# Gather, running sum and matrix product: sums and carry per tile of 128 rows in place of pairs of 256

## Chip, cores, metric

One core of one Trainium2 chip. The metric is the device time of one execution in microseconds (us), median of the runs of a kernel. The runs were spread over several chips, and the same kernel differs between them by up to 1.2%, so every kernel is compared only with runs of the kernel before on the same chip.

## The reference

```python
B, S, N, D = 16, 4096, 2048, 512
# x: (B, S, D) float32; indices: (B, N) sorted int64; w: (D, D) float32
def reference(x, indices, w):
    gathered = x[np.arange(B)[:, None], indices, :].copy()
    cs = np.cumsum(gathered, axis=1)
    return np.matmul(cs, w).astype(np.float32)
```

That is 16 x 2048 = 32768 gathered rows, 256 tiles of 128 rows, 128 pairs of tiles.

## The kernel before

Five engines work as a chain, each with its own list of instructions, coupled by semaphores:

- GpSimd gathers one tile of 128 rows per instruction (fp32 in HBM, fp16 in the core's memory) into a ring of 16 tiles. It may overwrite a pair's buffers when TensorE (PE) has signalled (`s_a`) that this pair's sums are done.
- PE multiplies the gathered tile with a triangle of ones. That gives the running sums within a tile or pair, already transposed (`sums`).
- VectorE adds the last column of the pair before to the sums and casts them to fp16 (`carry`, signal `s_d`).
- PE multiplies the carried sums with w (`project`, signal `s_b`).
- ScalarE copies the product out of PSUM (`drain`, signal `s_e`), and SyncE stores it.

Cuts from the kernel (its constants drawn together in the first line, comments added, left-out lines as `...`):

```python
R, NG, NA, NB, NC, NO, AH = 2, 16, 2, 2, 4, 8, 2   # AH: pairs that sums run ahead of project
...
def gather(t):
    g, r = divmod(t, R)
    pool.need(s_a, g + 1 - NG // R)            # wait: sums of the pair 8 earlier are done
    ...
    nc.gpsimd.indirect_dma_start(
        out=g16[g % (NG // R)][:, r, :], out_offset=None, in_=x_flat,
        in_offset=bass.IndirectOffsetOnAxis(ap=ap, axis=0),
        element_offset=(t // NT) * S * D,
    ).then_inc(s_g[t % NG], 16)

def sums(t):
    g, r = divmod(t, R)
    pe.need(s_g[t % NG], 16 * (t // NG + 1))
    pe.need(s_d, g - NA + 1)
    for c in range(DC):
        if r == 0 and c == 1:
            pe.need(s_e, g - AH - NB + 1)      # the drain of the pair four earlier
        mm = nc.tensor.matmul(
            out=pa[g % NA][:, c] if r == 0 else pa[g % NA][:, c, :, Q:],
            lhsT=g16[g % (NG // R)][:, r, c * P : (c + 1) * P],
            rhs=ut[:] if r == 0 else ut[:, :, :Q], ...)
    if r == R - 1:
        mm.then_inc(s_a, 1)
...
for g in range(1, G - AH - 1):                 # PE's steady loop
    for j in range(R):
        sums(R * (g + AH) + j)
        project(g, j)
```

The first tile of a pair writes 256 columns (both halves of the pair, since its rows count for all later ones), the second adds its 128. So a pair's sums are 4 x 256 + 4 x 128 = 1536 columns.

## Time and profile before

| | before |
|---|---|
| time, median of 3 | 404.81 us |
| span of the profiled run, mean granted clock | 403.2 us, 0.976 |
| PE busy | 324.4 us, 80% |
| GpSimd busy, all but 1.3 us of it gathers | 241.6 us, 60% |
| last gather issued | 375.57 us |

PE is the busiest engine, but a fifth of the span is not PE work.

### The profile page before, as it was taken

To read this page: it belongs to the slowest core of one execution; us is meant where nothing else is said; L and a number is where in the kernel's file an instruction comes from. 1 tells how busy PE (TensorE), PEld (TensorE's weight loads), DVE (VectorE), ACT (ScalarE), POOL (GpSimd) and SP (SyncE) were. 2 spreads that over 40 slices of the span, in tenths; PEclk is the share of its full clock that TensorE was granted. 3 is DMA by queue.
4 is the path that set the end of the run, shared out by engine and by line. 5 is a ranking of instruction groups with operands and counts; after the bars stand their busy time and mean duration, and the time that the engine had idled before them with its cause. 6 is when DMAs were issued, how large, how long until landed. Compare 5 with 4: busy or idle time off the path is not lost.

```text
span 403.2 us, 5096 instructions
## 1 busy us (share of the span) xinstructions
PE 324.4 (80%) x2064; PEld 182.4 (45%) x2064; DVE 159.2 (39%) x136; ACT 131.8 (33%) x132; POOL 241.6 (60%) x264
## 2 busy tenths in 40 slices
PE   5617988878888887888888788888878888888893
PEld 2303544444444444444444444444444444444451
DVE  2212443344444334434333443443344343433541
ACT  2102433333334333343333433343333333333442
POOL 6774666566666656666665666666566666666100
PEclk9867999999999999999999999999999999999998
DMA  7996999999999999999999999999999999999954
GB/s 175 140 128 111 278 262 262 280 272 270 259 283 257 272 269 269 279 255 284 256 275 264 278 268 266 277 258 271 267 278 271 257 284 264 277 251 281 287 227 191
DMA packets 56871, 102.32 MB, mean 254 GB/s; under 512 B 6800, under 2 KB 39824, under 8 KB 56848
## 3 DMA queue, kind: packets, MB, share of 16 engines
q0 software_dynamic: 36864, 33.57, 58.2%
q1 hardware_dynamic: 19712, 68.43, 44.2%
q8 instruction: 16, 0.26, 0.3%
q10 hardware_dynamic: 272, 0.00, 0.0%
q14 instruction: 7, 0.06, 0.0%
HBM read 68.42 MB, written 67.11 MB: 336 GB/s over the span
## 4 chain that ended last, share of the span: by engine, by line
PE 79%; issue 15%; DVE 2%; DMA 2%; ACT 0%; SPq 0%; ACTq 0%
PE pb L156 58%; PE pa L128 22%; DVE cst L146 2%; DMA g<-in_x_dram,idx_first 1%; DMA idx_first<-in_indices_dram 0%; ACT ob L168 0%; ACT ob L180 0%; ACTq L23 0%; SPq L332 0%; SPq L78 0%
## 5 line engine op out<-in xcount | busy, mean ns | idle before, releaser
L156 PE MATMUL pb<-w,cst 128*128 128x512 f16 x1024 | 266.7, 384 | 67.9 <-issue 56.6
L111 POOL DMA_INDIRECT g<-in_x_dram,idxg x252 | 236.4, 938 | 132.0 <-PE pa L128 66.3
L146 DVE TENSOR_TENSOR cst<-pa,cst 128x1024 f16<-128x1024 f32 x112 | 137.2, 1225 | 203.2 <-PE pa L128 144.8
L168 ACT COPY ob<-pb 128x1024 f32<-128x1024 f32 x127 | 128.5, 1012 | 261.9 <-remote 132.1
L156 PEld LDWEIGHTS pb<-w,cst 128*128 128x128 f16 x1024 | 94.1, 99 | 141.4 <-issue 65.8
L128 PE MATMUL pa<-ut,g 128*128 128x256 f16 (+1 forms) x1024 | 127.7, 248 | 4.3 <-DMA g<-in_x_dram,idx_first 2.7
L128 PEld LDWEIGHTS pa<-ut,g 128*128 128x128 f16 x1024 | 89.8, 99 | 69.4 <-issue 7.8
L142 DVE CAST cst<-pa 128x1024 f16<-128x1024 f32 x16 | 19.5, 1222 | 25.6 <-PE pa L128 18.4
L244 PE MATMUL pb<-zeros 128*128 128x512 f16 x14 | 5.2, 535 | 1.5 <-DVE zeros L248 1.5
L111 POOL DMA_INDIRECT g<-in_x_dram,idx_first x4 | 3.9, 986 | 2.0 <-DMA idx_first<-in_indices_dram 1.1
L244 PEld LDWEIGHTS pb<-zeros 128*128 128x128 f16 x14 | 1.7, 131 | 3.8 <-issue 1.9
L302 ACT CAST w<-w 128x512 f16<-128x512 f32 x2 | 1.2, 618 | 2.8 <-DMA w<-in_w_dram 2.8
L265 DVE CAST w<-w 128x512 f16<-128x512 f32 x2 | 0.9, 452 | 3.1 <-DMA w<-in_w_dram 3.1
L251 DVE CAST idxf<-idx 128x128 f32<-128x128 uint32 x2 | 0.5, 238 | 3.5 <-DMA idx<-in_indices_dram 3.5
L299 ACT ACT_TABLE_LOAD x1 | 1.3, 1283 | 1.5 <-SPq L78 1.5
L180 DVE COPY ob<-pb 128x512 f32<-128x512 f32 x1 | 0.7, 691 | 2.1 <-PE pb L156 2.1
L180 ACT COPY ob<-pb 128x512 f32<-128x512 f32 x1 | 0.6, 586 | 0.7 <-PE pb L156 0.7
L248 DVE MEMSET zeros<- 128x256 uint32 x1 | 0.3, 272 | 1.1 <-SPq L78 1.1
L256 PEld LDWEIGHTS pb<-ident,idxf 128*128 128x128 f32 x2 | 0.4, 187 | 0.6 <-DVE idxf L251 0.3
L262 DVE CAST idxg<-pb 128x128 uint32<-128x128 f32 x2 | 0.5, 292 | 0.2 <-PE pb L256 0.2
L256 PE MATMUL pb<-ident,idxf 128*128 128x128 f32 x2 | 0.5, 303 | 0.0
L215 POOL MEMSET ident<- 128x128 f32 x1 | 0.2, 205 | 0.5 <-SPq L78 0.5
(8 smaller groups left out, 1.6 us busy)
## 6 DMA issues: line engine op xcount, KB each, us to landing
out_dram<-ob SPq DMA_DIRECT2D x127, 512.0 KB
g<-in_x_dram,idxg POOLq DMA_INDIRECT x252
w<-in_w_dram SPq DMA_DIRECT2D x4, 256.0 KB
out_dram<-ob SPq DMA_DIRECT2D x2, 256.0 KB, 2.7
idx<-in_indices_dram SPq DMA_DIRECT2D x2, 128.0 KB, 2.6
g<-in_x_dram,idx_first POOLq DMA_INDIRECT x4
idx_first<-in_indices_dram ACTq DMA_DIRECT2D x1, 2.0 KB, 2.2
idx_first<-in_indices_dram SPq DMA_DIRECT2D x1, 2.0 KB, 2.0
```

The source lines that it names most:

```text
L111: nc.gpsimd.indirect_dma_start(out=g16[g % (NG // R)][:, r, :], out_offset=None, in_=x_flat, in_offset=bass.IndirectOffsetOnAxis(ap=ap, ax ...
L128: mm = nc.tensor.matmul(out=pa[g % NA][:, c] if r == 0 else pa[g % NA][:, c, :, Q:], lhsT=g16[g % (NG // R)][:, r, c * P : (c + 1) * P], r ...
L142: nc.vector.tensor_copy(out=dst[:], in_=pa[g % NA][:]).then_inc(s_d, 1)
L146: nc.vector.tensor_tensor(out=dst[:], in0=pa[g % NA][:], in1=last.unsqueeze(2).broadcast_to([P, DC, R, P]), op=mybir.AluOpType.add,).then_ ...
L156: mm = nc.tensor.matmul(out=pb[g % NB][:, j], lhsT=cst[g % NC][:, c, j, :], rhs=w16[:, c, :], start=(c == 0), stop=(c == DC - 1),)
L168: nc.scalar.copy(out=ob[g % NO][:], in_=pb[g % NB][:]).then_inc(s_e, 1)
L180: copy(out=ob[g % NO][:, j], in_=pb[g % NB][:, j]).then_inc(s_el[j], 1)
L244: nc.tensor.matmul(out=pb[NB - 1][:, R - 1], lhsT=zeros[:, :P], rhs=zeros[:], start=True, stop=True)
L256: nc.tensor.transpose(out=pb[k % NB][:, 0, :P], in_=idxf[:, k, :], identity=ident[:]).then_inc(s_pt, 1)
L265: nc.vector.tensor_copy(out=w16[:, c, :], in_=w32[:, c, :]).then_inc(s_wc, 1)
L299: nc.scalar.copy(out=spare[:], in_=zeros[:, :1])
L302: nc.scalar.copy(out=w16[:, c, :], in_=w32[:, c, :]).then_inc(s_wc, 1)
```

## The change

The intent is to stream fewer columns on PE. If each tile is summed on its own, the first tile of a pair no longer has to write its sums into the second tile's half: its four matmuls have 128 columns in place of 256. VectorE then carries tile by tile (twice as many adds of half the size), and the two PSUM buffers for sums become four of half the size. The core of the diff:

```diff
-    NA = 2
+    NA = 4
-    ut = const.tile([P, R, P], FP16)
+    ut = const.tile([P, R, Q], FP16)
-    pa = [ps.tile([P, DC, R, P], FP32, name=f"pa{i}") for i in range(NA)]
+    pa = [ps.tile([P, DC, R, Q], FP32, name=f"pa{i}") for i in range(NA)]
...
     def gather(t):
-        pool.need(s_a, g + 1 - NG // R)
+        pool.need(s_a, R * (g + 1) - NG)
...
     def sums(t):
-        pe.need(s_d, g - NA + 1)
+        pe.need(s_d, t - NA + 1)
...
-                out=pa[g % NA][:, c] if r == 0 else pa[g % NA][:, c, :, Q:],
+                out=pa[t % NA][:, c],
-                rhs=ut[:] if r == 0 else ut[:, :, :Q],
+                rhs=ut[:],
...
-        if r == R - 1:
-            mm.then_inc(s_a, 1)
+        mm.then_inc(s_a, 1)
-    def carry(g):
-        dve.need(s_a, g + 1)
+    def carry(t):
+        g, r = divmod(t, R)
+        dve.need(s_a, t + 1)
+        dst = cst[g % NC][:, :, :, r * Q : (r + 1) * Q]
...
     def project(g, j):
-        pe.need(s_d, min(g + 1 + j, G) if g else 1)
+        pe.need(s_d, min(R * (g + 1) + j, T))
```

More of the change, by code (lines that the diff above doesn't have):

```diff
@@ L54 @@
     AH = 2
-    assert R == 2 and D == 512 and N % (R * P) == 0 and T % P == 0
+    assert D == 512 and N % (R * P) == 0 and T % P == 0
     x_flat = x.rearrange("b s d -> (b s) d")
@@ L128, in sums @@
             mm = nc.tensor.matmul(
-                out=pa[g % NA][:, c] if r == 0 else pa[g % NA][:, c, :, Q:],
+                out=pa[t % NA][:, c],
                 lhsT=g16[g % (NG // R)][:, r, c * P : (c + 1) * P],
-                rhs=ut[:] if r == 0 else ut[:, :, :Q],
-                start=(r == 0 and c * R * P % D == 0),
-                stop=(r == R - 1 and (c + 1) * R * P % D == 0),
-            )
-        if r == R - 1:
-            mm.then_inc(s_a, 1)
-    def carry(g):
-        dve.need(s_a, g + 1)
-        dst = cst[g % NC]
-        if g % GB == 0:
-            nc.vector.tensor_copy(out=dst[:], in_=pa[g % NA][:]).then_inc(s_d, 1)
+                rhs=ut[:],
+                start=(c == 0),
+                stop=(c == DC - 1),
+            )
+        mm.then_inc(s_a, 1)
[3 more added lines that the diff above has]
+        dst = cst[g % NC][:, :, :, r * Q : (r + 1) * Q]
+        if t % NT == 0:
+            nc.vector.tensor_copy(out=dst, in_=pa[t % NA][:]).then_inc(s_d, 1)
             return
-        last = cst[(g - 1) % NC][:, :, R - 1, P - 1 : P]
-        dve.need(s_d, g)
+        e = (r - 1) % R
+        last = cst[(t - 1) // R % NC][:, :, R - 1, e * Q + Q - 1 : e * Q + Q]
+        dve.need(s_d, t)
         nc.vector.tensor_tensor(
-            out=dst[:],
-            in0=pa[g % NA][:],
-            in1=last.unsqueeze(2).broadcast_to([P, DC, R, P]),
+            out=dst,
+            in0=pa[t % NA][:],
+            in1=last.unsqueeze(2).broadcast_to([P, DC, R, Q]),
             op=mybir.AluOpType.add,
@@ L232 @@
         base=0,
-        pattern=[[1, R], [R, P]],
+        pattern=[[1, R], [R, Q]],
         channel_multiplier=-1,
@@ L265 @@
         nc.vector.tensor_copy(out=w16[:, c, :], in_=w32[:, c, :]).then_inc(s_wc, 1)
-    for g in range(G):
-        carry(g)
+    for t in range(T):
+        carry(t)
     drain_last(0, dve, nc.vector.tensor_copy)
```

## The prediction

> **What bounds the kernel now.** I read the page first (busy shares, chain, costliest groups), then the groups with shapes kept apart, then the timelines of single engines over one repeat of the steady state, then two stretches compared.
>
> ```profile
> PE 324.4 (80%) x2064; PEld 182.4 (45%) x2064; DVE 159.2 (39%) x136; ACT 131.8 (33%) x132; POOL 241.6 (60%) x264
> PE 79%; issue 15%; DVE 2%; DMA 2%; ACT 0%; SPq 0%; ACTq 0%
> ```
>
> PE is the busiest engine and 79% of the chain, yet 15% of the chain is "issue": PE idle for no reason that the profile names. So streaming columns are not all of the time. From the groups:
>
> ```profile
> L156 PE MATMUL pb<-w,cst 128*128 128x512 f16 x1024 | 266.7, 384 | 67.9 <-issue 56.6 <-DVE cst L146 11.2
> L111 POOL DMA_INDIRECT g<-in_x_dram,idxg x252 | 236.4, 938 | 132.0 <-PE pa L128 66.3 <-issue 65.7
> L146 DVE TENSOR_TENSOR cst<-pa,cst 128x1024 f16<-128x1024 f32 x112 | 137.2, 1225 | 203.2 <-PE pa L128 144.8 <-issue 41.9 <-remote 13.0
> L128 PE MATMUL pa<-ut,g 128*128 128x256 f16 x512 | 78.5, 276 | 4.1 <-DMA g<-in_x_dram,idx_first 2.7 <-issue 1.2
> L128 PE MATMUL pa<-ut,g 128*128 128x128 f16 x512 | 49.5, 219 | 0.2 <-issue 0.2
> ```
>
> PE's idle time stands before the projections (67.9 us), none before the sums: gathered data is always there in time. Where it falls is in PE's timeline, one repeat:
>
> ```profile
> 205.50 1.04 PE L156 MATMUL pb<-w,cst 128*128 128x512 f16 x4 [1.47 <-issue]
> ...
> 207.68 0.39 PE L128 MATMUL pa<-ut,g 128*128 128x128 f16 x4
> ...
> 210.06 0.39 PE L128 MATMUL pa<-ut,g 128*128 128x128 f16 x4
> ...
> 212.45 0.39 PE L128 MATMUL pa<-ut,g 128*128 128x128 f16 x4
> 214.30 1.04 PE L156 MATMUL pb<-w,cst 128*128 128x512 f16 x4 [1.47 <-issue]
> ```
>
> Every 8.79 us, which is three pairs of tiles (48 matmuls), PE stops for 1.46 us. The groups of four at 207.68, 210.06 and 212.45 end the sums of three pairs. VectorE's timeline for the same stretch:
>
> ```profile
> 208.10 1.23 DVE L146 TENSOR_TENSOR cst<-pa,cst 128x1024 f16<-128x1024 f32 x1 [1.33 <-PE pa L128]
> 213.02 1.23 DVE L142 CAST cst<-pa 128x1024 f16<-128x1024 f32 x1 [3.70 <-PE pa L128]
> 214.35 1.23 DVE L146 TENSOR_TENSOR cst<-pa,cst 128x1024 f16<-128x1024 f32 x1
> ```
>
> The first pair's carry starts 0.03 us after its sums end (208.07). The second pair's sums end at 210.45, but its carry starts at 213.02, with VectorE idle in between: PE's completion signal came 2.57 us late. ScalarE's drain, due at 211.32, starts at 213.13: late too. PE ran on until the projection that needs that carry, waited for it (213.02 + 1.23 = 214.25) and resumed at 214.30. GpSimd's timeline:
>
> ```profile
> 210.68 0.94 POOL L111 DMA_INDIRECT g<-in_x_dram,idxg  x1 [0.30 <-issue]
> 213.26 0.94 POOL L111 DMA_INDIRECT g<-in_x_dram,idxg  x1 [1.64 <-PE pa L128]
> 214.50 0.94 POOL L111 DMA_INDIRECT g<-in_x_dram,idxg  x1 [0.30 <-issue]
> ```
>
> It issues six gathers, one each 1.243 us, starves for buffers because the same signals are late, and starts again when they come. So the cycle also reads 6 x 1.243 + 1.33 = 8.79 us. Does gathering have to do with the lateness? The last gather is issued at 375.57; the two stretches before and after:
>
> ```profile
> 56.00:375.40 319.40, 266.95 (x1745) 152.33 (x1746) 133.31 (x110) 110.31 (x109) 204.46 (x218) 1.00 1.09 269
> 375.40:393.00 17.60, 17.60 (x114) 10.10 (x115) 8.40 (x7) 7.54 (x8) 0.94 (x1) 1.00 0.74 252
> ```
>
> The first two figures are the length and PE's busy time. With gathers PE is busy 84%, without them 100%, at the same full clock (1.00) and with the same semaphores between PE, VectorE and ScalarE; a pair takes 319.4 / 109 = 2.93 us with them and 2.39 us without. The late signals come with gather issue. Why, the trace does not say.
>
> [...] four of 128 take 0.39 us at 219 ns each, so they start (390-219)/3 = 57 ns apart; four of 512, (1030-379)/3 = 217. Weight loads do not show through.
> [...]the trace has one 128x512 PSUM copy on VectorE, 691 ns[...]
> [...] Here the bubble is fed by late signals, and buffers set how far an engine gets before it notices.
>
> **The change part by part.**
> Sums: per pair, four matmuls of 256 columns become 128; the other four stay. At 109 against 56 ns apart that is 4 x 0.053 = 0.21 us per pair, 27 us over 128 pairs; a pair's PE work goes from 2.39 to 2.17 us.
> Carry: 128 adds of 1.225 us become 256 of about 0.69: 1.38 us per pair in place of 1.23, on an engine 39% busy: free. A single carry is 0.53 us shorter, so PE is released earlier after a late signal.
> Signals: PE posts three completions per pair (two sums, one projection) instead of two.
> Buffers: [...] The sums of a tile reach the projection that needs them after three projections and three sums of 128 columns, 3 x 0.86 + 3 x 0.22 = 3.3 us, where before it was 2.4. The output side is unchanged: two projection buffers, drained in 1.01 us. From the end of a projection to the sums that need its buffer free there are now 2.2 us of PE work (before 2.5), so a drain signal late by more than 2.2 - 1.2 = 1.0 us still stops PE; it was late by 1.8.
> Gathers: the same 256, gated as before by whole pairs.
>
> Sum, as I believe it: the cycle is closed through GpSimd. A burst of gathers runs as long as there are freed buffers; signals of PE that end 4.5 us or less after the burst starts pass, the one at 6.0 us does not, and the release comes 1.36 us after the burst's last gather. With k pairs in a cycle, a pair takes 2 x 1.243 + 1.33/k. For k = 3 that is 2.93, as measured, and nothing in it is PE streaming. In the new kernel PE resumes about 1.2 us after the release, ends pairs at about 2.5, 4.6 and 6.8 us after it, and stops at about 7.7 for the drain: again two pairs before the block and one in it, k = 3. Then the 0.21 us per pair becomes longer idling, except in the last ten pairs (no gathers): 404.8 - 10 x 0.21 = 402.6 us.
>
> **The rivals.**
> (1) PE streaming is the bound and the stall stays a fixed cost: all 27 us are gained, 377 us. For it: PE's 79% of the chain. Against: the 1.33 us that GpSimd would no longer have; 6 gathers need 7.46 us and the PE part would be 3 x 2.17 + 1.46 = 7.97.
> (2) The release is caused by PE running dry (it comes about 0.14 us after PE's last matmul, as regularly as 1.36 us after the last gather). Then earlier carries pay too: 3 x 2.17 + about 1.0 = 7.5 us, 2.5 per pair, 109 x 0.43 = 47 us less: 356. Against: at 27.2 and 317.0 us signals came through with PE long idle, or running.
> (3) A fourth pair fits before the block: 2.487 + 1.33/4 = 2.82, 109 x 0.11 + 2 = 14 us less: 391.
> (4) What blocks is the number of signals, three passing per cycle in the trace; with three per pair instead of two the block comes a pair earlier. With k = 2, 3.15 per pair: +24 - 2 us, 427; with k between 2 and 3, 3.02: 412. For it: the signals are what is late, and the change makes half again as many of them. Against: in the last stretch they flow freely.
>
> **Range and chances.** Unchanged at about 403 is likeliest; (4) I hold likelier than (1), (2) and (3) together, since the trace shows signals and not columns to be short. Weighed: 405 us, range 380 to 428; faster by over 2% (below 396.7) 0.25, within 2% 0.40, slower (above 412.9) 0.35.
>
> **What would show it.** Steps right: groups of sum matmuls all of 128 columns, starting 56 ns apart; carries near 0.69 us; GpSimd still in bursts of six with 1.3 us between; PE's idle time before L156 and L128 grown by about 20 us; the stretch after the last gather at 2.17 us per pair. Wrong: bursts of another length (k of 4 or 2 gives rivals 3 or 4), a cycle shorter than 7.8 us (rival 2), or no stalls at all, which would mean that finer signals are not held and the gathers' 318 us become the floor.

The sum came to 404.8 - 10 x 0.21 = 402.7 us (recorded as 402.6), and its figures can be read from the trace of the kernel before. There the next matmul starts 109 ns after a sum of 256 columns, 56 ns after one of 128 and 216 ns after a projection, in the median, so 0.053 us is 109 less 56 ns. The 0.69 us for a carry is the 691 ns of the one 128x512 copy out of PSUM (L180). That weight loads do not show through is this: one takes 99 ns in the mean, yet sums start 56 ns apart, and in 375.40:393.00 PE is busy throughout while weight loads take 10.10 us.

## The result

The changed kernel took 401.86 us (four runs, 401.70 to 403.29), the kernel before beside it 404.85 us (404.65 to 405.32). The ratio is 0.9932, with a 95% interval of 0.9908 to 0.9956: the same within 2%, slightly faster. A ratio here is the mean time of one kernel's runs over that of the other's runs of the same rounds, so it is not quite the ratio of the medians quoted.

The page of the changed kernel: the line of busy times and the line of the chain by engine ("another core or an unknown queue" is waiting whose end the profile could not put down to anything).

```profile
PE 322.6 (81%) x2064; PEld 167.6 (42%) x2064; DVE 178.9 (45%) x264; ACT 128.4 (32%) x132; POOL 241.5 (60%) x264
PE 74%; issue 10%; another core or an unknown queue 7%; ACT 4%; DMA 2%; DVE 1%; ACTq 0%; DVEq 0%; SPq 0%
```

A third of the columns of the sums are gone, 512 matmuls x 0.053 us (spacings of 109 and 56 ns) = 27 us of streaming, and PE's busy time is 1.8 us shorter. The costliest groups on the same page (busy us, mean ns of one | idle us before them) say where it went:

```profile
L156 PE MATMUL pb<-w,cst 128*128 128x512 f16 x1024 | 285.3, 405 | 16.1 <-DVE cst L146 15.1
L146 DVE TENSOR_TENSOR cst<-pa,cst 128x512 f16<-128x512 f32 x240 | 166.1, 692 | 197.7 <-PE pa L127 116.4
...
L127 PE MATMUL pa<-ut,g 128*128 128x128 f16 x1024 | 114.2, 229 | 54.9 <-issue 37.8
```

The sums (L127) are now 1024 equal matmuls. The projections (L156) have not been touched, and yet one takes 405 ns in the mean in place of 384: they run more often at a granted clock of 0.50 (its mean over the span is 0.917, before 0.976). The idle time moved from before the projections (67.9 us before) to before the sums (54.9 us), but its total is the same: stops of over 0.15 us add up to 70.8 us, before 71.8. GpSimd's timeline over one repeat (start us, length us, engine, line, operation, [idle us before <- what ended it]):

```profile
196.09 0.94 POOL L111 DMA_INDIRECT g<-in_x_dram,idxg  x1 [1.67 <-remote]
...
201.06 0.94 POOL L111 DMA_INDIRECT g<-in_x_dram,idxg  x1 [0.31 <-issue]
202.30 0.94 POOL L111 DMA_INDIRECT g<-in_x_dram,idxg  x1 [0.30 <-issue]
204.88 0.94 POOL L111 DMA_INDIRECT g<-in_x_dram,idxg  x1 [1.64 <-remote]
```

The burst that starts at 196.09 has six gathers again, 1.243 us apart, and the next starts at 204.88, 8.79 us later: the cycle of the kernel before to 0.01 us. 36 bursts of six are in the trace, in both kernels. VectorE's timeline shows why GpSimd starves:

```profile
201.80 0.69 DVE L146 TENSOR_TENSOR cst<-pa,cst 128x512 f16<-128x512 f32 x1 [2.07 <-PE pa L127]
204.65 3.08 DVE L146 TENSOR_TENSOR cst<-pa,cst 128x512 f16<-128x512 f32 x4 [2.16 <-remote]
```

and PE's timeline, what it does to PE:

```profile
203.61 0.22 PE L127 MATMUL pa<-ut,g 128*128 128x128 f16 x1
205.83 0.34 PE L127 MATMUL pa<-ut,g 128*128 128x128 f16 x3 [1.99 <-ACT ob L168]
206.01 1.03 PE L156 MATMUL pb<-w,cst 128*128 128x512 f16 x4
...
207.20 1.91 PE L156 MATMUL pb<-w,cst 128*128 128x512 f16 x4
```

PE ended the sums of three tiles at 200.63, 201.83 and 202.91 us, but VectorE got no signal between 201.8 and 204.6 us, and then carried all that had piled up. It is the signals that are late, not VectorE that is slow to act on them: the packed trace also records when `s_a` was raised, and for these three tiles it was at 204.62, 204.74 and 204.84 us. Before, one carry (1.23 us) stood between the late signal and PE's next projection; now PE stops in the middle of the sums, after the first of a tile's four matmuls, where it waits for a drain (`s_e`) that waits for one of the same late signals. The stop is 2.0 us in place of 1.46 us, and soon after it the granted clock goes from 1.00 to 0.50 (at 206.96 us): from 207.20 us four projections take 1.91 us in place of 1.03. At the clock of 0.50 the next matmul starts about 427 ns after a projection in place of 216; 97 projections have such a spacing, before 17, and (97 - 17) x 0.21 = 17 us. With the sums, matmuls in the half-clock stretches lose 25.9 us against full-clock spacing, before 5.2 us. So about 21 of the 27 us that were saved are spent in the slower clock. Some 3 us more go in spacings that are longer at full clock, and 3 us are gained.

After which stops the clock fell can be read from the record of the granted clock, which in both traces changes in steps of 3.41 us. Two such steps (length, busy us of PE, the weight loads, VectorE, ScalarE and GpSimd, granted clock, DMA share, GB/s):

```profile
203.55:206.96 3.41, 1.42 (x12) 0.67 (x10) 2.08 (x3) 1.93 (x2) 1.77 (x2) 1.00 1.07 250
206.96:210.38 3.42, 3.42 (x16) 1.70 (x15) 1.39 (x2) 1.01 (x1) 2.50 (x4) 0.50 1.09 304
```

Between 56 and 376 us the changed kernel has 13 stretches at 0.50, each one step long. None of its stops there is over 2.31 us. In the step before each of them PE was idle for 1.98 us or more; in the steps that full clock followed, for at most 2.00 us. In the kernel before no step of that stretch has more than 1.56 us of idle time, and its clock stays at 1.00.

Two stretches, one with gathers and one after the last gather (length, then busy us of PE, of the weight loads, of VectorE, ScalarE and GpSimd, granted clock, DMA share, GB/s):

```profile
56.00:376.20 320.20, 267.93 (x1741) 139.98 (x1740) 149.31 (x217) 107.28 (x110) 204.29 (x218) 0.93 1.08 268
376.20:393.00 16.80, 16.80 (x119) 9.14 (x117) 10.38 (x15) 7.82 (x8) 0.94 (x1) 1.00 0.84 294
```

With 16 matmuls to a pair, the first stretch takes 320.2 x 16 / 1741 = 2.94 us per pair (before, the same way, 2.93). Nothing was gained there, and the clock went from 1.00 to 0.93. The last gather is issued at 376.38 us, 0.8 us later than before. From then to the end it takes 23.6 us, before 27.6: the whole gain is in the tail.

### The profile page after: what moved, and what is told of

Same layout as the page of the kernel before. It is cut to its first block, busy times and chain, and to the rows that moved or that the text cites. A ratio compares the mean times of both kernels' runs of the same rounds, so it can differ in the third digit from the quotient of the medians.

```text
span 400.0 us, 5354 instructions
## 1 busy us (share of the span) xinstructions
PE 322.6 (81%) x2064; PEld 167.6 (42%) x2064; DVE 178.9 (45%) x264; ACT 128.4 (32%) x132; POOL 241.5 (60%) x264
## 3 DMA queue, kind: packets, MB, share of 16 engines
q0 software_dynamic: 36864, 33.57, 59.2%
## 4 chain that ended last, share of the span: by engine, by line
PE 74%; issue 10%; another core or an unknown queue 7%; ACT 4%; DMA 2%; DVE 1%; ACTq 0%; DVEq 0%; SPq 0%
PE pb L156 57%; PE pa L127 17%; ACT ob L168 4%; DVE cst L146 1%; DMA g<-in_x_dram,idx_first 1%; DMA idx_first<-in_indices_dram 0%; ACT ob L180 0%; ACTq L23 0%; DVEq L23 0%; SPq L332 0%; SPq L78 0%
## 5 line engine op out<-in xcount | busy, mean ns | idle before, releaser
L156 PE MATMUL pb<-w,cst 128*128 128x512 f16 x1024 | 285.3, 405 | 16.1 <-DVE cst L146 15.1
L146 DVE TENSOR_TENSOR cst<-pa,cst 128x512 f16<-128x512 f32 x240 | 166.1, 692 | 197.7 <-PE pa L127 116.4
L168 ACT COPY ob<-pb 128x1024 f32<-128x1024 f32 x127 | 125.1, 1014 | 262.2 <-PE pb L156 183.7
L127 PE MATMUL pa<-ut,g 128*128 128x128 f16 x1024 | 114.2, 229 | 54.9 <-issue 37.8
L127 PEld LDWEIGHTS pa<-ut,g 128*128 128x128 f16 x1024 | 81.0, 103 | 134.6 <-issue 70.2
L156 PEld LDWEIGHTS pb<-w,cst 128*128 128x128 f16 x1024 | 94.6, 103 | 88.0 <-DVE cst L146 17.1
L141 DVE CAST cst<-pa 128x512 f16<-128x512 f32 x16 | 10.9, 684 | 10.0 <-PE pa L127 10.0
L180 DVE COPY ob<-pb 128x512 f32<-128x512 f32 x1 | 0.7, 692 | 1.3 <-PE pb L156 1.3
L180 ACT COPY ob<-pb 128x512 f32<-128x512 f32 x1 | 0.6, 585 | 0.9 <-PE pb L156 0.9
```

Of the source, the lines that this page charges most:

```text
L127: mm = nc.tensor.matmul(out=pa[t % NA][:, c], lhsT=g16[g % (NG // R)][:, r, c * P : (c + 1) * P], rhs=ut[:], start=(c == 0), stop=(c == DC ...
L141: nc.vector.tensor_copy(out=dst, in_=pa[t % NA][:]).then_inc(s_d, 1)
L146: nc.vector.tensor_tensor(out=dst, in0=pa[t % NA][:], in1=last.unsqueeze(2).broadcast_to([P, DC, R, Q]), op=mybir.AluOpType.add,).then_inc ...
L156: mm = nc.tensor.matmul(out=pb[g % NB][:, j], lhsT=cst[g % NC][:, c, j, :], rhs=w16[:, c, :], start=(c == 0), stop=(c == DC - 1),)
L168: nc.scalar.copy(out=ob[g % NO][:], in_=pb[g % NB][:]).then_inc(s_e, 1)
L180: copy(out=ob[g % NO][:, j], in_=pb[g % NB][:, j]).then_inc(s_el[j], 1)
```

## Experiments

Theory A: while GpSimd issues gathers one after the other, completion signals of PE are held up. The steady cycle is closed through that: GpSimd issues what PE's signals freed, the signals come when GpSimd stops. PE's own streaming is not in it. The rivals, each put to a run: PE's streaming does count (B in the expectations); GpSimd's wait on PE's semaphore is the cause (A2); the number of signals is; the DMA traffic is; any work of GpSimd is; the buffers are too few.

"Late" below means that an engine starts more than 0.5 us after both the recorded end of the PE matmul that it waits for and the end of its own work before; such cases are counted from the timelines of VectorE and ScalarE. In the kernel before 42 of 128 carries and 42 drains are late, in the changed one 82 of 256 carries and 64 drains.

### No gathers after the first sixteen, in both kernels

```diff
-        pe.need(s_g[t % NG], 16 * (t // NG + 1))
+        pe.need(s_g[t % NG], 16)
...
-    for t in range(T):
+    for t in range(NG):
         gather(t)
```

PE sums the first sixteen tiles again and again; the result is wrong.

> The changed kernel with the first 16 gathers alone; later tiles reuse their data (wrong result on purpose). Stores, sums, carries, projections and their signals stay. Theory A: PE's signals are late only while gathers are issued, so no bubbles from the start: 128 x 2.17 = 278 us of PE plus about 12 at the start and 8 at the end, about 298 us, PE over 95% busy. If the lateness comes from the number of signals or from the stores: bubbles stay, 360 us or more.

> The kernel before with the first 16 gathers alone (wrong result on purpose). Theory A: PE bound without bubbles, 128 x 2.39 = 306 us plus about 20: about 326 us, so 27 us or 9% slower than the changed kernel without gathers: what the change saves on PE, seen where PE is the bound. If bubbles stay: 380 us or more, and no such difference.

Measured: the changed kernel 307.42 us (307.14 to 309.09), the kernel before 335.6 us (334.49 to 336.81). The line of busy times, first of the changed kernel without gathers:

```profile
PE 289.0 (95%) x2064; PEld 161.1 (53%) x2064; DVE 179.8 (59%) x264; ACT 131.8 (43%) x132; POOL 16.3 (5%) x24
```

and of the kernel before without gathers:

```profile
PE 317.0 (95%) x2064; PEld 182.6 (55%) x2064; DVE 159.8 (48%) x136; ACT 131.9 (40%) x132; POOL 16.5 (5%) x24
```

No drain is late; of the carries four and two are, all before 26 us, while the first sixteen gathers are issued or just done. Both kernels took 9 to 10 us more than expected. The change is worth 28 us here, as its columns say (27 us): with PE as the bound it works. And with gathers the changed kernel takes 94 us more, although the only wait of PE for gathered data in its profile is one of 1.9 us, before the first sums.

### The saved columns streamed again

The sums of the first tile of each pair are done twice, so that PE streams as many columns as in the kernel before, with all else as in the changed one.

```diff
-        for c in range(DC):
-            if r == 0 and c == 1:
+        for n in range(2 * DC if r == 0 else DC):
+            c = n % DC
+            if r == 0 and n == 1:
                 pe.need(s_e, g - AH - NB + 1)
```

> The changed kernel, with the four sum matmuls of the first tile of each pair streamed twice (same result), so that PE streams as many columns per pair as before the change. Theory A (the cycle is closed through GpSimd: bursts of six gathers and 1.33 us of idling, 8.79 us per three pairs, whatever PE streams): steady state unchanged, only the some ten pairs after the last gather pay 0.22 us each: about 404 us, PE idle time falls by about 25 us. Theory B (PE's columns are the bound and the stall a fixed addition): 128 x 0.22 = 28 us more, about 430 us.

Measured: 407.5 us (407.09 to 407.96), ratio 1.0061 (1.0045 to 1.0078) to the kernel before, thus 1.3% over the changed kernel. 512 further matmuls of 56 ns are 29 us; the time moves by about 5. That PE's streaming is the bound is refuted. But the cycle is not untouched either, as theory A had it: it was to stay, and the time to be 404 us. GpSimd's timeline:

```profile
198.58 0.94 POOL L111 DMA_INDIRECT g<-in_x_dram,idxg  x1 [0.30 <-issue]
200.77 0.94 POOL L111 DMA_INDIRECT g<-in_x_dram,idxg  x1 [1.25 <-PE pa L128]
```

The bursts are now of four gathers (54 of them), with 1.25 us between: two pairs in 5.9 us, 2.96 us per pair. Another rhythm with nearly the same rate; signals are late here too (115 carries and 109 of 127 drains). The granted clock is back at 0.968; PE's stops are 0.95 us here.

### GpSimd gated by another engine

GpSimd waits for ScalarE's drains in place of PE's sums, so that it reads none of PE's semaphores.

```diff
-        pool.need(s_a, R * (g + 1) - NG)
+        pool.need(s_e, g + 1 - NG // R)
```

> The changed kernel with GpSimd's gathers waiting for ScalarE's drain signal of the pair eight pairs back in place of PE's sums signal (two to three pairs stricter). Theory A1 (issuing gathers is enough to hold PE's signals up): about the same cycle, 400 to 410 us. Theory A2 (they are held because GpSimd itself waits for PE's semaphore): bubbles vanish, gathers flow at 1.243 us each, 318 us plus 20: about 340 us.

Measured: 425.33 us, ratio 1.0492 (1.0467 to 1.0516). 79 carries and 43 drains are late, the drains by 3.3 us in the median. Bubbles did not vanish, so GpSimd's wait on PE's semaphore is not the cause. But the time is outside the 400 to 410 us of A1 as well. The likely reason, not tested, is that a buffer is now freed by a drain, which itself waits for a late signal of PE.

### Two signals per pair in place of three

PE signals only after the second tile of each pair.

```diff
-        mm.then_inc(s_a, 1)
+        if r == R - 1:
+            mm.then_inc(s_a, 1)
...
-        pool.need(s_a, R * (g + 1) - NG)
+        pool.need(s_a, g + 1 - NG // R)
...
-        dve.need(s_a, t + 1)
+        dve.need(s_a, g + 1)
...
-        pe.need(s_d, min(R * (g + 1) + j, T))
+        pe.need(s_d, min(R * (g + 1) + (j if g else 0), T))
```

> The changed kernel, but PE signals only after the second tile of each pair, so two signals a pair as in the kernel before (the carries of both tiles wait for it). Theory A (while GpSimd issues gathers back to back, PE's signals are held, whatever their number): bursts of six, a cycle of about 8.8 us per three pairs, 402 us (398 to 406). Rival 4 of the prediction (what blocks is a number of signals): with two instead of three per pair the block comes later, bursts of eight or more, 2.82 us per pair or less, 391 us or less.

Measured: 406.67 us against 409.69 on that chip, ratio 0.9933 (0.9916 to 0.9949), which is the changed kernel's own ratio; 37 bursts of six. A third fewer signals change nothing: rival 4 of the prediction falls, and with it its reason for a slower result.

### What in a gather does it: traffic, work, or issue?

Three runs with the changed kernel. Their outputs are wrong, which doesn't matter for the times. First, traffic without GpSimd: no gathers after sixteen, and the same bytes read into spare buffers by transfers from ScalarE's queue.

```diff
+    def load(g):
+        act.need(s_j[g % 8], 16 * (g // 8))
+        rows = x_flat[g * R * P : (g + 1) * R * P, :].rearrange("(p j) d -> p j d", j=R)
+        nc.scalar.dma_start(out=junk[g % 8][:], in_=rows).then_inc(s_j[g % 8], 16)
...
         drain(g)
+        if NG // R <= g + 8 < G:
+            load(g)
```

> The changed kernel without gathers after the first sixteen (the old tiles are summed again, so the result is wrong on purpose), but with the same number of bytes read from the same tensor into spare buffers, 256 rows of 2 KB per pair, by transfers that ScalarE's queue issues. Theory A (GpSimd's issuing holds the signals, not the bytes that move): as without gathers, 307 us (305 to 315), PE 95% busy, under ten late carries. Rival (the traffic of the DMA engines itself delays the signals): 360 us or more, PE under 85% busy.

Measured: 347.56 us (two runs, 349.28 and 345.84), between the two expectations. Two carries are late. 88 drains are, but for another reason, which two lines of the page name (the group of drains; the issues of stores with KB each and us to landing):

```profile
L170 ACT COPY ob<-pb 128x1024 f32<-128x1024 f32 x127 | 128.6, 1013 | 199.1 <-DMA out_dram<-ob 137.4
...
out_dram<-ob SPq DMA_DIRECT2D x127, 512.0 KB, 19.2
```

The drains wait for stores that take 19.2 us. The loads arrive as fp32 (62.9 MB in place of the gathers' 33.6), and the DMA engines move 418 GB/s in place of the 268 GB/s of the changed kernel. This run is bound by transfers, so it does not give the price of traffic; but with half as much again of it, PE's signals to VectorE are on time.

Second, work on GpSimd without issue: a memset of about a gather's length in the place of each gather, under the same waits.

```diff
         pool.need(s_a, R * (g + 1) - NG)
+        if t >= NG:
+            fill_one(t - NG)      # memset of a 128x896 tile, four tiles in turn
+            return
```

> The changed kernel without gathers after the first sixteen (wrong on purpose), but with a memset on GpSimd of about 1 us in the place of each gather, gated by the same signals. Theory A [...]: 307 us (305 to 315), under ten late carries. Rival (any back-to-back work of GpSimd under these waits does it): stops of PE of 1 to 2 us in each cycle, 370 us or more.

Measured: 307.51 us (308.3 and 306.72), as without gathers. Two carries and one drain are late.

```profile
L106 POOL MEMSET fill<- 128x896 f32 x240 | 195.6, 845 | 62.6 <-PE pa L136 62.6
```

240 memsets of 0.85 us, and GpSimd waits for PE as it should. Here work on GpSimd and its waits don't hold the signals. Third, issue almost without traffic: each gather fetches 64 columns of its 128 rows.

```diff
-            out=g16[g % (NG // R)][:, r, :],
+            out=g16[g % (NG // R)][:, r, : D if t < NG else 64],
-            in_=x_flat,
+            in_=x_flat if t < NG else x_flat.rearrange("n (k d) -> (n k) d", d=64),
```

> The changed kernel with each gather after the first sixteen fetching 64 columns of a row in place of 512 (wrong on purpose): as many gathers, as many rows and issues by GpSimd, an eighth of the bytes. Theory A (the issuing of gathers by GpSimd holds PE's signals): nothing changes much, 395 to 403 us, bursts of six with 1.3 us and more between, over 70 late carries. Rival (the gathers' own traffic on the DMA engines, which with the stores are about 100% busy in the page, does it): 305 to 340 us, few late carries, GpSimd at one gather per 1.24 us or waiting for buffers that PE frees at 2.2 us per pair.

Measured: 406.94 us (two runs) against 409.52 on that chip, ratio 0.9937 (0.9916 to 0.9959), again the ratio of the changed kernel. 36 bursts of six, 80 late carries. The queue of the gathers on its page (packets, MB, share of 16 engines' span):

```profile
q0 software_dynamic: 36864, 6.05, 19.6%
```

In the changed kernel this share is 59.2%, and the bytes are 33.57 MB. With as many issues and packets but under a fifth of the bytes, the time is the same. Of the three, then, it is the issuing of gathers by GpSimd, 128 rows each, that goes with the late signals.

The runs alone leave a rival: the many packets of the gathers (36864 in both; the loads above came in 17552), and the gathers' own completion signals (`s_g`). The traces speak against it. Each gather has 144 packets (36864 / 256), 128 of them of 1024 bytes and 16 of 4 bytes in the changed kernel. When the signals came at 204.62 us in the changed kernel, 372 packets of the gathers already issued had still to end; when they came at 198.2 us with narrow gathers, 17. Yet from the end of a burst's last gather instruction to the first late start of VectorE or ScalarE it is 1.4 us in the one and 1.5 us in the other, in the median of 36 bursts each. So the release does not wait for the packets, nor for the gathers' own signals: in the changed kernel some `s_g` of gathers already issued are recorded at 204.70 us and later. Nor do VectorE and GpSimd just get in each other's way: 64 of ScalarE's drains are late too.

### Spacing the gathers

The result stays right: after each pair of gathers GpSimd does a memset of 128x512, 128x256 or 128x128.

```diff
     for t in range(T):
         gather(t)
+        if t % R == R - 1 and t >= NG:
+            fill_one((t - NG) // R)
```

> The changed kernel, right result, with a memset of 128x512 on GpSimd after the two gathers of each pair, which spaces the gathers (by an estimated 0.4 to 0.9 us per pair, from the 0.20 us that a memset of 128x128 took). Theory A with the addition that a signal is only held as long as one gather follows the other at once: signals pass in every pause, under 30 late carries, no stops of 2 us; then GpSimd's own pace is the floor, 2.49 + pause per pair, about 2.9 to 3.4 us, 390 to 440 us. Rival (the pauses do not help, signals are let through only when GpSimd waits for PE): bursts as before but longer, late carries over 70, 410 us or more.

> As the run with a memset of 128x512 after each pair of gathers, but 128x256, about 0.31 us (worked out from 0.20 us for 128 columns and 0.541 for 512). In the run before, GpSimd's own rhythm of 2.90 us per pair was the floor (pauses of 0.70 us, hardly ever longer) though signals were late by up to 4.8 us. Theory P (with a pause after each pair the signals get through fast enough for GpSimd to stay the floor): the rhythm becomes 2.36 + 0.31 = 2.67 us per pair, 120 x 0.23 = 27 us less than the 406.7 us of that run's profile, about 380 us, pauses in GpSimd of 0.48 us nearly all. Rival Q (the shorter the pause, the fewer signals get through, and the freed buffers become the floor again): pauses of 1 us or more come back in GpSimd every few pairs, and the time is between 392 and 405 us.

> The same with a memset of 128x128, 0.20 us: Theory P: 2.36 + 0.20 = 2.56 us per pair, 40 us less than with 512 columns, about 367 us. Rival Q: as the changed kernel without any pause, 398 to 405 us, bursts of about six gathers with 1.3 us or more between them.

| memset after each pair | ratio to before (95%) | mean pause between a pair's gathers and the next pair's | late carries |
|---|---|---|---|
| none (changed kernel) | 0.9932 (0.9908 to 0.9956) | 0.75 us | 82 |
| 128x128, 0.22 us | 0.9955 (0.9939 to 0.9972) | 0.75 us | 90 |
| 128x256, 0.33 us | 0.9931 (0.9915 to 0.9948) | 0.75 us | 113 |
| 128x512, 0.54 us | 0.9966 (0.9946 to 0.9986), two runs | 0.80 us | 142 |

The pauses are counted from the end of a pair's second gather to the start of the next gather, whatever fills them, as the mean of 116 pauses after the first burst. Part of my addition to theory A fell: with a pause of 0.70 us after every pair, 142 carries are still late, not under 30; only each lateness is shorter (0.83 us in the median against 2.16). And the times of the two shorter memsets are those of rival Q. What the pauses show instead is nearly the same mean. GpSimd's timeline with the memset of 128x256:

```profile
197.64 0.33 POOL L106 MEMSET fill<- 128x256 f32 x1
199.21 0.95 POOL L117 DMA_INDIRECT g<-in_x_dram,idxg  x1 [1.23 <-PE pa L133]
...
201.89 0.95 POOL L117 DMA_INDIRECT g<-in_x_dram,idxg  x1 [0.16 <-issue]
```

Most pauses are 0.49 us, and every fourth grows to 1.5 us until the mean is 0.75 us, as in the changed kernel, where two pauses of 0.30 us and one of 1.64 us give the same. A pair's two gathers take 2.19 us with the 0.30 us between them, and 2.19 + 0.75 = 2.94. In these four runs it does not matter whether the time without gathers is spread or in one piece, and giving up to 0.54 us of it per pair as work to GpSimd costs next to nothing. But the mean pause is only the time per pair less those 2.19 us: that it is the same says no more than that the times are. It is no constant of the chip (0.98 us with GpSimd gated by drains), and what sets 2.94 us per pair is not shown.

In these traces the late signals also don't come at any time: between one late signal's arrival and the next one's lie 0.7, 1.4, 2.1 or 2.8 us, to within 0.15 us, in most cases (with 128x512, counting starts over 0.3 us late: 72, 69, 30 and 8 of 229 intervals). Where the 0.7 us come from is not shown.

### Twice as many gather buffers

```diff
-    NG = 16
+    NG = 32
```

> The changed kernel with 32 gathered tiles in place of 16. The prediction's reading (the cycle is set by how far PE gets on signals that were let through, and GpSimd issues as many gathers as PE freed): after a longer first burst the same cycle of 8.8 us per three pairs, 402 us (398 to 407). Rival (too few gather buffers make the bubble): GpSimd no longer starves, 390 us or less.

Measured: 423.2 us (421.87 to 424.61) against 409.52, ratio 1.0324 (1.0295 to 1.0353). Slower, which neither side expected. The steady cycle is the expected one, 36 bursts of six; the loss is at the start, where GpSimd now has 38 gathers to issue before it must wait for PE. VectorE's timeline in that stretch:

```profile
13.75 0.69 DVE L146 TENSOR_TENSOR cst<-pa,cst 128x512 f16<-128x512 f32 x1 [2.48 <-issue]
16.97 0.69 DVE L146 TENSOR_TENSOR cst<-pa,cst 128x512 f16<-128x512 f32 x1 [2.53 <-PE pa L127]
20.53 0.69 DVE L146 TENSOR_TENSOR cst<-pa,cst 128x512 f16<-128x512 f32 x1 [2.87 <-PE pa L127]
26.13 0.69 DVE L146 TENSOR_TENSOR cst<-pa,cst 128x512 f16<-128x512 f32 x1 [4.91 <-remote]
34.58 0.69 DVE L146 TENSOR_TENSOR cst<-pa,cst 128x512 f16<-128x512 f32 x1 [7.76 <-remote]
54.88 0.69 DVE L146 TENSOR_TENSOR cst<-pa,cst 128x512 f16<-128x512 f32 x1 [19.61 <-remote]
```

VectorE carries one tile each 3.2, 3.6, 5.6, 8.5 and at last 20.3 us, ever more slowly the longer the burst lasts. The last gather of the burst ends at 50.67 us, and 4.2 us later the signals arrive. PE stands still for 22 us of it, waiting for a drain:

```profile
59.48 0.50 PE L127 MATMUL pa<-ut,g 128*128 128x128 f16 x3 [22.15 <-ACT ob L168]
```

This is the clearest view of the hold: gathers run without a pause, and PE's signals dry up. The time is 3.9% over the changed kernel's (1.0324 / 0.9932). The PSUM buffers, for whose drain PE waits, were not made more.

In the changed kernel the first burst has 22 gathers and costs in the same way. Sixteen further buffers cost (1.0324 - 0.9932) x 409.5 = 16 us, about 1 us each; eight fewer might therefore save some 8 us. That is an estimate from the start alone, and whether the steady cycle would bear it is open; it was not tried.

## Why the prediction was right, and where not

The prediction was 405.0 us, from a derived 402.6 us (its sum 404.8 - 2.1 gives 402.7) and its rivals; measured were 401.86 us. The stated 405.0 is the derived time pulled up by the weight of rival 4, for which the runs give no support. And the derived time is near in part because two errors pull against each other: the tail gained more than derived, and the last gather came later. Point by point:

- **The cycle is closed through GpSimd, k = 3.** Right: bursts of six, 8.79 us, 2.94 us per pair in the changed kernel, and PE stops for the drain, as derived. The run with the columns streamed again shows that PE's columns do not set the rate, though they changed the rhythm to bursts of four.
- **Release 1.36 us after a burst's last gather.** Right here: the last gather ends at 203.24 and VectorE starts at 204.65, so the signal came at about 204.6. It is no constant, though: about 1.0 us after bursts of four, 4.2 us after the burst of 38. And that signals that end 4.5 us or less after the burst's start pass was too tidy: in the burst that starts at 196.09 the sums that ended at 199.55 us, 3.5 us in, were signalled at 201.78, 2.2 us late. As k = 3 was derived with this rule, it came out right partly by luck.
- **Rival 1 (streaming is the bound, 377 us)** is refuted by the columns streamed again, rival 2 (release by PE running dry, 356 us) by the release 0.8 us after PE ran dry at 203.83, where before it was 0.14 us, with the same distance from the last gather, rival 3 (k = 4) by the count of bursts, rival 4 (the number of signals, 412 to 427 us) by two signals per pair in place of three. I had held rival 4 likelier than the other three together; the run gives no support for that.
- **The columns become idle time, about 20 us more of it.** Wrong. PE's idle time fell by 1 us; the projections went from 384 to 405 ns in the mean, as the granted clock fell from 0.976 to 0.917 with stops of 2.0 us. The time is the same, since PE was not in the cycle, but the step named the wrong place.
- **Sums 56 ns apart, carries 0.69 us.** Right: four sums take 0.39 us at 222 ns, so they start (390 - 222) / 3 = 56 ns apart, and a carry takes 692 ns.
- **The last stretch at 2.17 us per pair, ten pairs, 2.1 us gained.** The rate is right (carries at 385.15 and 387.32 us, one pair apart). The gain of the tail was mis-sized: 27.6 - 23.6 = 4.0 us, of which 0.8 us is lost again since the last gather comes later. By the records after the last gather: 24 narrower matmuls in place of ten pairs' 40, 24 x 0.053 = 1.3 us; PE being eight matmuls further on at that time, 4 x 0.216 + 4 x 0.109 = 1.3 us; and 1.3 us for a stop that the prediction had overlooked, together 3.9 us. In the kernel before, PE waits 1.32 us near the end for the last carry of 1.23 us; with carries of half the size nothing waits there.

What stays open: why PE's signals are held while GpSimd issues gathers. Shown are that gathers issued by GpSimd go with it and that their bytes, GpSimd's other work, its waits and the number of PE's signals do not; that the hold is longest in the longest burst (carries up to 20.3 us apart in the one of 38 gathers); that it goes for PE's signals to VectorE and ScalarE, while in the trace of before SyncE's stores start 0.03 us after the drains and PE resumes 0.06 us after the carry that it waits for, both in the median. The mechanism is not shown.

## What to carry to other kernels

When the busiest engine stops in a regular cycle, look first at which engine's rhythm the period is made of. That the period can be summed up from one engine's steps is a hint and no proof; here streaming the saved columns again, 29 us of work that moved the time by 5, was the test. Do not take it that a signal arrives when its work ends (here one came 2.57 us later): compare the recorded end of the work with the start of what waits for it. And in a kernel that gathers from GpSimd, more buffers can hurt (sixteen more: ratio 1.0324 in place of 0.9932): long uninterrupted bursts of gathers here cost 22 us of standstill, and fewer, not more, should be the next trial.
